# A low-half score product on 64 partitions instead of 128

## Chip, cores and metric

One Trainium2 chip, one core. The time is device microseconds of one launch, the median of several runs; lower is better. All matrix products run on TensorE (PE in the profile, its weight loads PEld), everything elementwise on VectorE (DVE), ScalarE (ACT) and GpSimd (POOL); transfers are queued by SyncE (SP).

## What is computed

A decoder trunk of two layers over 1024 tokens of width 1024. Each layer has a mixer (RMSNorm, one input projection, dilated sliding-window attention beside stick-breaking attention, gates, output projection) and a gated feed-forward block. The edit lies in the dilated attention: twelve heads of width 64 in three groups with (window, dilation) of (128, 1), (512, 4) and (2048, 16).

```python
DSW_GROUPS = ((128, 1), (512, 4), (2048, 16))
DSW_HEADS_PER_GROUP = 4
...
scores = jnp.einsum('brhnqc,brhnkc->brhnqk', qs, kw).astype(jnp.float32) * (hd ** -0.5)
...
scores = jnp.where(valid, scores + bias, -jnp.inf)
mx = jnp.max(scores, axis=-1, keepdims=True)
p = jnp.exp(scores - mx)
den = jnp.sum(p, axis=-1, keepdims=True)
o = jnp.einsum('brhnqk,brhnkc->brhnqc', p, vw) / den
```

The score product contracts over c, the head width of 64.

## The kernel before

All products are made in a rounded fp32 type (F32R) from a high and a low part: a number x is split into hi, the rounded value, and lo = x - hi, and a product is hi·hi + hi·lo + lo·hi. For dense products these are three matmuls (lines 1014 to 1016, for example). For scores, where only 64 of the 128 partitions would be filled, two parts share one matmul. The helper `scores(o, qt, ql, k)` (line 643) makes two matmuls into the same PSUM tile: its first (line 644) takes as k a tile with k's high part on partitions 0 to 63 and k's low part on 64 to 127, and as qt the high part of q on both halves, so that it sums hi·hi and hi·lo; its second (line 645) takes the low part of q on partitions 0 to 63 and zeros on 64 to 127, so that it adds lo·hi. The first argument behind the output is the stationary operand (128 partitions x 128 columns, loaded by an LDWEIGHTS record), k is the moving one.

Three kinds of attention item call this helper: `stick_item` (stick-breaking), `near_item` (dilation 1) and `far_item` (the two dilated groups together). The last is the one concerned. There are 16 far items a layer (i from 0 to 15), each for one head slot and one residue of the sequence, with both groups g = 0, 1. Their operands lie in a tile `t_kq` of shape [128, g, 3, 256]; the middle index is k (0), q high (1), q low (2). Two such tiles alternate (`R["kq", i % 2]`). `fetch_kq(i)` (line 866) fills one from a scratch tensor `tk` in HBM with three transfers on SP's queue: one for partitions 0 to 63 (line 872: k high, q high, q low) and one for each group on partitions 64 to 127 (line 874: k low, q high). The third column block of partitions 64 to 127 is never transferred. It is set to zero by a memset on POOL (line 870), once for each of the two tiles, in the first two fetches of a layer.

The function `score` inside `far_item` (line 889) makes an item's eight matmuls one behind the other, with nothing between them: for each g the pair of lines 644 and 645 on 128 key columns into bank z0 (line 899), then for each g the pair on 256 key columns into bank z1 (line 901). VectorE then adds the bias and takes the maximum (line 913, read as a minimum since signs are turned), ScalarE exponentiates (line 914). Later calls transpose the probabilities (lines 921 to 923) and multiply by the values (lines 931 and 933).

TensorE's list is written by hand order: `manual_schedule` keeps the order of the program text. A generator object `Dense` holds the layer's dense products (projections for gates, q, k and v: lines 1014 to 1016) and hands them out in between; `attend` calls an item's score, then dense pieces, then its transposes and value products, at a fixed rate for each kind of item. So the order on TensorE is fixed when the program is built. `fetch` asks for t_kq of item i when item i - 2 has been scored. Two further lines matter as a comparison: line 2120 transposes five small parameter arrays of 8, 16, 66, 22 and 8 rows once a layer, and line 839 transposes a tile of 32 columns.

Of the kernel before, what the change touches and what calls it, by code (L numbers as in the profile page):

```python
# [16 lines left out]
P = 128  # L17
# [39 lines left out]
def f32(ap):  # L57
    return ap.bitcast(F32)
# [3 lines left out]
def trunk_kernel(ctx, tc, x, norm1, w_in, b_gate, w_br, w_o, norm2, w_up, conv_w, conv_b, w_down, norm_f, out, depth=None, probe=None):  # L62
    nc = tc.nc
    act, dve, pe, pool = nc.scalar, nc.vector, nc.tensor, nc.gpsimd
# [60 lines left out]
    def bank(tag, name):  # L125
        return ps.tile([P, 512], F32, tag=tag, name=name)
# [95 lines left out]
    class Dense:  # L222
# [43 lines left out]
        def fetch(self):  # L266
# [28 lines left out]
            while self.kq < self.scored + 2 and there(self.kq):  # L295
                fetch_kq(self.kq)
                self.at(LEAD_T if self.kq > 1 else LEAD - 2 * self.kq, lambda i=self.kq: self.done.add(f"F{i}"))
                self.kq += 1
# [343 lines left out]

    def scores(o, qt, ql, k):
        pe.matmul(o, qt, k, start=True, stop=False, skip_group_check=True)
        pe.matmul(o, ql, k, start=False, stop=True, skip_group_check=True)

    def parts(src, n, name):

        hi, lo = small(name + "h", F32R), small(name + "l", F32R)
        with tc.high_priority(offset=AHEAD):  # L650
            split(hi[:, :n], lo[:, :n], src[:, :n], "is")
        return hi, lo

    def fold(dst, o):

        n = o.shape[-1]
        tmp = small("fold")
        with tc.high_priority(offset=AHEAD):
            act.copy(tmp[0:64, :n], o[64:128, :])
            dve.tensor_tensor(dst, o[0:64, :], tmp[0:64, :n], ALU.add)  # L660
# [205 lines left out]
    def fetch_kq(i):  # L866

        if i < 2:
            t = R["kq", i] = sb.tile([P, 2, 3, 256], F32R, tag="xa", bufs=4, name="t_kq")
            pool.memset(f32(t[64:128, :, 2, :]), 0.0)  # L870
        t, there = R["kq", i % 2], tk[i // 8][i // 4 % 2, :, i % 4]
        nc.sync.dma_start(f32(t[0:64]), there[:, :, 1:4, :])
        for g in range(2):
            nc.sync.dma_start(f32(t[64:128, g, 0:2, :]), there[:, g, 0:3:2, :])
# [5 lines left out]
    def far_item(dense, pr, s, r, share):  # L880
        i = 8 * pr + 4 * s + r
        slot = 2 * pr + s
        if s == 0 and r == 0:
            R["st1", pr] = sb.tile([P, 2, 2, 2, 4], F32, tag="st1", bufs=2, name="st1")
            R["ot", pr] = None
        st = R["st1", pr]
        shared = {}

        def score():
            if r == 0:  # L890
                bias = share["bias"] = sb.tile([P, 2, 256], F32, tag="bias", name="bias1")
                dve.tensor_scalar(bias[:, 0, :], base0, 4.0 * SLOPES[4 + slot], None, ALU.mult)
                dve.tensor_scalar(bias[:, 1, :], base2, 4.0 * SLOPES[8 + slot], None, ALU.mult)
            bias = share["bias"]
            pt = shared["p"] = sb.tile([P, T], F32, tag="p4", bufs=4, name="p1")
            z0, z1 = bank("s", "z10"), bank("s", "z11")
            t = R["kq", i % 2]
            for g in range(2):
                scores(z0[:, P * g : P * g + P], t[:, g, 1, 0:P], t[:, g, 2, 0:P], t[:, g, 0, 0:P])
            for g in range(2):  # L900
                scores(z1[:, 256 * g : 256 * g + 256], t[:, g, 1, P:256], t[:, g, 2, P:256], t[:, g, 0, :])
            dense.scored = i + 1
            if (s, r) == (1, 0):
                near_stats(pr)
            for n in range(2):
                flat = pt[:, 256:768] if n else pt[:, 0:256]
                if n:
                    zz, pp, bb = z1, flat, bias.rearrange("p g c -> p (g c)")
                else:
                    zz, pp, bb = z0[:, 0:256].rearrange("p (g c) -> p g c", g=2), flat.rearrange("p (g c) -> p g c", g=2), bias[:, :, P:256]  # L910
                nm = st[:, 0, s, n, r : r + 1]
                with tc.high_priority(offset=AHEAD):
                    LAST["red"] = dve.tensor_tensor_reduce(pp, zz, bb, 1.0, 3e38, ALU.add, ALU.min, nm).ins.name
                    act.activation(flat, flat, AF.Exp, bias=nm, scale=-1.0, accum_out=st[:, 1, s, n, r : r + 1])
            if (s, r) == (1, 3):
                factors(pr)

        def turn(g):
            pt = shared["p"]
            tp = bank("t", "t1")  # L920
            pe.transpose(tp[:, 0:P], pt[:, P * g : P * g + P], ident)
            pe.transpose(tp[:, P : 2 * P], pt[:, 256 + 256 * g : 384 + 256 * g], ident)
            pe.transpose(tp[:, 2 * P : 3 * P], pt[:, 384 + 256 * g : 512 + 256 * g], ident)
            shared[g] = parts(tp, 384, "p1")

        def apply(g):
            if r % 2 == 0 and g == 0:
                share["o"] = bank("o", "o1")
            o, oc, vt = share["o"], 256 * (r % 2), R["v", i][:, g]
            for p in (0, 1):  # L930
                pe.matmul(o[:, oc : oc + 256], vt[:, 0:P], shared[g][p][:, 0:256], start=(r % 2 == 0 and g == 0 and p == 0), stop=False, skip_group_check=True)
            for p in (0, 1):
                pe.matmul(o[:, oc + P : oc + 256], vt[:, P:256], shared[g][p][:, 256:384], start=False, stop=(r % 2 == 1 and g == 1 and p == 1), skip_group_check=True)
            if g == 1:
                dense.applied = i + 1
            if r % 2 == 1 and g == 1:
                if R["ot", pr] is None:
                    R["ot", pr] = sb.tile([P, T], F32, tag="ot", name="ot")
                fold(R["ot", pr][64 * s : 64 * s + 64, 512 * (r // 2) : 512 * (r // 2) + 512], o)
                if s == 1 and r == 3:  # L940
                    join(dense, pr)

        return [score], [(lambda g=g: turn(g), lambda g=g: apply(g)) for g in range(2)]

    def near_stats(pr):
        sn = R["sn", pr] = sb.tile([P, 2, 2, 2, 4], F32, tag="sn", bufs=1, name="sn")
        nc.sync.dma_start(sn.rearrange("j a s n r -> j (a s) n r"), tok_view(dn[pr]))

    def factors(pr):

        sn, st = R["sn", pr], R["st1", pr]
        nat, far_ = (t.rearrange("j a s n r -> j a (s n r)") for t in (sn, st))
        w = sb.tile([P, 6, 16], F32, tag="sw", bufs=1, name="sw")
        f = R["f", pr] = sb.tile([P, 2, 2, 2, 4], F32, tag="sf", bufs=1, name="sf")
        ff = f.rearrange("j a s n r -> j a (s n r)")
        dve.tensor_tensor(w[:, 0, :], nat[:, 0, :], far_[:, 0, :], ALU.min)
        dve.tensor_tensor(w[:, 1, :], w[:, 0, :], nat[:, 0, :], ALU.subtract)
        dve.tensor_tensor(w[:, 2, :], w[:, 0, :], far_[:, 0, :], ALU.subtract)
        act.activation(w[:, 1:3, :], w[:, 1:3, :], AF.Exp)
        dve.tensor_tensor(w[:, 3, :], w[:, 1, :], nat[:, 1, :], ALU.mult)  # L960
        dve.tensor_tensor(w[:, 4, :], w[:, 2, :], far_[:, 1, :], ALU.mult)
        dve.tensor_tensor(w[:, 3, :], w[:, 3, :], w[:, 4, :], ALU.add)
        dve.reciprocal(w[:, 5, :], w[:, 3, :])
        dve.tensor_tensor(ff[:, 0, :], w[:, 1, :], w[:, 5, :], ALU.mult)
        dve.tensor_tensor(ff[:, 1, :], w[:, 2, :], w[:, 5, :], ALU.mult)

        R["fx", pr] = []
        for a in range(2):
            fx = sb.tile([P, 2, 4, 2, 64], F32, tag="p4", bufs=4, name="fx")
            for s in range(2):  # L970
                act.copy(fx[:, :, :, s, :], f[:, a, s, :, :].unsqueeze(3).to_broadcast([P, 2, 4, 64]))
            R["fx", pr].append(fx.rearrange("p n r s c -> p n r (s c)"))
# [1178 lines left out]
```

## Time and profile before

| | us |
|---|---|
| median of 3 runs (2620.66 to 2622.22) | 2621.4 |
| profiled execution, own time | 2621.54 |
| its span, first to last instruction | 2619.8 |

The profile is one execution. It lists, for each engine, instructions with start and length. A matmul's record runs from its start to a modelled end and overlaps those of its neighbours, so distances between starts tell more than lengths. In a record like "128*128 128x256" the first pair is rows x columns of the stationary operand, the second the moving one. "q<-p" names the tile written and those read; "<-" behind an idle time names what ended it. TensorE's clock as granted is 1.00 over the whole span.

### The profile page before, as it was taken

To read this page: it belongs to the slowest core of one execution; us is meant where nothing else is said; L and a number is where in the kernel's file an instruction comes from. 1 tells how busy PE (TensorE), PEld (TensorE's weight loads), DVE (VectorE), ACT (ScalarE), POOL (GpSimd) and SP (SyncE) were. 2 spreads that over 40 slices of the span, in tenths; PEclk is the share of its full clock that TensorE was granted. 3 is DMA by queue.
4 is the path that set the end of the run, shared out by engine and by line. 5 is a ranking of instruction groups with operands and counts; after the bars stand their busy time and mean duration, and the time that the engine had idled before them with its cause. 6 is when DMAs were issued, how large, how long until landed. Compare 5 with 4: busy or idle time off the path is not lost.

```text
span 2619.8 us, 36195 instructions
## 1 busy us (share of the span) xinstructions
PE 2606.3 (99%) x12732; PEld 2185.4 (83%) x12732; DVE 2089.1 (80%) x3485; ACT 1358.8 (52%) x2533; POOL 100.4 (4%) x135
## 2 busy tenths in 40 slices
PE   9999999999999999999999999999999999999999
PEld 8888888888888888888888888888888888888887
DVE  8877777795988888897677778777869888889965
ACT  6555666574554555422445555666645555544225
POOL 3000000030000000000000000000300000000000
PEclk9999999999999999999999999999999999999999
DMA  7434578873344444688344436787633344446962
GB/s 255 152 117 135 163 202 219 212 245 93 93 145 154 143 169 137 240 325 311 145 150 141 129 124 187 198 224 212 209 97 116 129 156 150 147 167 257 347 240 112
DMA packets 400418, 468.22 MB, mean 179 GB/s; under 512 B 24309, under 2 KB 315501, under 8 KB 398445
## 3 DMA queue, kind: packets, MB, share of 16 engines
q1 hardware_dynamic: 400220, 465.90, 55.1%
q8 instruction: 101, 1.65, 0.3%
q14 instruction: 81, 0.66, 0.1%
q10 hardware_dynamic: 16, 0.00, 0.0%
HBM read 303.23 MB, written 162.59 MB: 178 GB/s over the span
## 4 chain that ended last, share of the span: by engine, by line
PE 94%; DVE 2%; ACT 2%; DMA 1%; issue 1%; SPq 0%; POOL 0%; DVEq 0%; ACTq 0%; POOLq 0%
PE u_a L1014 6%; PE u_a L1016 6%; PE u_a L1015 6%; PE d_ps L1763 5%; PE d_ps L1764 5%; PE d_ps L1765 5%; PE i_a L1014 5%; PE i_a L1016 4%; PE i_a L1015 4%; PE u_c L1014 3%; PE u_c L1016 3%; PE u_c L1015 3%; PE i_c L1014 2%; PE i_c L1016 2%; PE i_c L1015 2%; PE o_ps L182 2%
## 5 line engine op out<-in xcount | busy, mean ns | idle before, releaser
L141 ACT CAST w_hi<-up_a 128x512 fp32r<-128x512 f32 x280 | 174.0, 622 | 277.1 <-DVE up_a L1617 120.6
L148 DVE TENSOR_TENSOR w_lo<-up_a,w_hi 128x512 fp32r<-128x512 f32 x280 | 189.6, 689 | 83.4 <-ACT w_hi L141 83.4
L141 ACT CAST w_hi<-in_a 128x512 fp32r<-128x512 f32 x252 | 156.1, 622 | 163.4 <-PE i_c L1015 38.3
L148 DVE TENSOR_TENSOR w_lo<-in_a,w_hi 128x512 fp32r<-128x512 f32 x252 | 173.0, 688 | 74.9 <-ACT w_hi L141 65.8
L1771 DVE TENSOR_TENSOR x<-x,d_ps 128x512 f32<-128x512 f32 (+1 forms) x228 | 153.8, 676 | 64.9 <-PE d_ps L1765 61.5
L1763 PE MATMUL d_ps<-gd_in,w_hi 128*128 128x512 f32 (+1 forms) x340 | 130.1, 383 | 0.0
L1764 PE MATMUL d_ps<-gd_in,w_hi 128*128 128x512 f32 (+1 forms) x340 | 129.9, 382 | 0.0
L1765 PE MATMUL d_ps<-gd_in,w_lo 128*128 128x512 f32 (+1 forms) x340 | 129.9, 382 | 0.0
L1014 PE MATMUL u_a<-t_hi,w_hi 128*128 128x512 f32 x320 | 124.6, 389 | 0.0
L1016 PE MATMUL u_a<-t_hi,w_lo 128*128 128x512 f32 x320 | 124.6, 389 | 0.0
L1015 PE MATMUL u_a<-t_lo,w_hi 128*128 128x512 f32 x320 | 124.6, 389 | 0.0
L1016 PE MATMUL u_a<-hh,w_lo 128*128 128x512 f32 x320 | 124.6, 389 | 0.0
L1014 PE MATMUL u_a<-hh,w_hi 128*128 128x512 f32 x320 | 124.6, 389 | 0.0
L1015 PE MATMUL u_a<-hl,w_hi 128*128 128x512 f32 x320 | 124.6, 389 | 0.0
L1014 PE MATMUL i_a<-hh,w_hi 128*128 128x512 f32 x288 | 119.2, 414 | 0.0
L1014 PE MATMUL i_a<-t_hi,w_hi 128*128 128x512 f32 x288 | 118.4, 411 | 0.0
L1763 PE MATMUL d_ps<-gd_in,wd 128*128 128x512 f32 (+1 forms) x292 | 114.0, 390 | 0.0
L1016 PE MATMUL i_a<-hh,w_lo 128*128 128x512 f32 x288 | 113.2, 393 | 0.0
L1016 PE MATMUL i_a<-t_hi,w_lo 128*128 128x512 f32 x288 | 113.1, 393 | 0.0
L1015 PE MATMUL i_a<-t_lo,w_hi 128*128 128x512 f32 x288 | 113.0, 392 | 0.0
L1765 PE MATMUL d_ps<-gd_in,wd 128*128 128x512 f32 (+1 forms) x292 | 112.9, 387 | 0.0
L1764 PE MATMUL d_ps<-gd_in,wd 128*128 128x512 f32 (+1 forms) x292 | 112.9, 387 | 0.0
(379 smaller groups left out, 7839.6 us busy)
## 6 DMA issues: line engine op xcount, KB each, us to landing
gd<-g SPq DMA_DIRECT2D x154, 512.0 KB, 3.3
gd_in<-gd SPq DMA_DIRECT2D x154, 512.0 KB, 6.2
up_a<-in_w_up_dram SPq DMA_DIRECT2D x80, 512.0 KB, 5.3
in_a<-in_w_in_dram SPq DMA_DIRECT2D x72, 512.0 KB, 5.4
wd_raw<-in_w_down_dram SPq DMA_DIRECT2D x22, 1024.0 KB, 11.2
gin<-gs SPq DMA_DIRECT2D x32, 512.0 KB, 4.3
w_raw<-in_w_o_dram SPq DMA_DIRECT2D x64, 256.0 KB, 2.9
gs<-u SPq DMA_DIRECT2D x48, 256.0 KB, 4.0
```

What stands on the lines that cost most here:

```text
L141: one = act.copy(hi, src)
L148: two = dve.tensor_tensor(lo, src, f32(hi), ALU.subtract)
L182: pe.matmul(o, lh, rh, start=(first and i == 0), stop=False, skip_group_check=share)
L1014: pe.matmul(o, w[0][:, c], rh, start=(first and i == 0), stop=False, skip_group_check=True)
L1015: pe.matmul(o, w[0][:, c], rl, start=False, stop=False, skip_group_check=True)
L1016: pe.matmul(o, w[1][:, c], rh, start=False, stop=(last and i == 3), skip_group_check=True)
L1763: pe.matmul(o[:, sub], wh[:, c], gh[:, sub], start=(i == 0 and k in (0, 4, 5)), stop=False, skip_group_check=True)
L1764: pe.matmul(o[:, sub], wh[:, c], gl[:, sub], start=False, stop=False, skip_group_check=True)
L1765: pe.matmul(o[:, sub], wl[:, c], gh[:, sub], start=False, stop=(i == m - 1), skip_group_check=True)
L1771: dve.tensor_tensor(x, x, o[:, sub], ALU.add)
```

## The change

The second matmul of `scores` takes as many partitions of k as its stationary operand has. The far items hand in q's low part on partitions 0 to 63 alone, so their second product contracts over 64 partitions. The zeros beside it are no longer read, and the memset is left out. The other two kinds of item still hand in 128 partitions. Later line numbers go down by one.

```diff
     def scores(o, qt, ql, k):
         pe.matmul(o, qt, k, start=True, stop=False, skip_group_check=True)
-        pe.matmul(o, ql, k, start=False, stop=True, skip_group_check=True)
+        pe.matmul(o, ql, k[0 : ql.shape[0]], start=False, stop=True, skip_group_check=True)
...
             t = R["kq", i] = sb.tile([P, 2, 3, 256], F32R, tag="xa", bufs=4, name="t_kq")
-            pool.memset(f32(t[64:128, :, 2, :]), 0.0)
...
             for g in range(2):
-                scores(z0[:, P * g : P * g + P], t[:, g, 1, 0:P], t[:, g, 2, 0:P], t[:, g, 0, 0:P])
+                scores(z0[:, P * g : P * g + P], t[:, g, 1, 0:P], t[0:64, g, 2, 0:P], t[:, g, 0, 0:P])
             for g in range(2):
-                scores(z1[:, 256 * g : 256 * g + 256], t[:, g, 1, P:256], t[:, g, 2, P:256], t[:, g, 0, :])
+                scores(z1[:, 256 * g : 256 * g + 256], t[:, g, 1, P:256], t[0:64, g, 2, P:256], t[:, g, 0, :])
```

## The prediction

> **What bounds the kernel now.** I read the page first: busy times, the granted clock, and the chain of waits that ended last.
>
> ```profile
> span 2619.8 us, 36195 instructions
> PE 2606.3 (99%) x12732; PEld 2185.4 (83%) x12732; DVE 2089.1 (80%) x3485; ACT 1358.8 (52%) x2533; POOL 100.4 (4%) x135
> PEclk9999999999999999999999999999999999999999
> PE 94%; DVE 2%; ACT 2%; DMA 1%; issue 1%; SPq 0%; POOL 0%; DVEq 0%; ACTq 0%; POOLq 0%
> ```
>
> TensorE sets the end: busy 99% of the span, 94% of the chain, at full clock. That average need not hold where the edit lies, so the table by stretches came next, cut at the first and the last score product of the dilated heads in each layer.
>
> ```profile
> 412.40:495.10 82.70, 81.83 (x486) 70.85 (x485) 61.27 (x135) 50.28 (x115) 0.52 (x1) 1.00 0.87 220
> 1705.80:1814.90 109.10, 107.10 (x639) 92.98 (x638) 79.92 (x179) 63.80 (x149) 0.52 (x1) 1.00 0.85 216
> ```
>
> The columns are length, then busy time of PE, PEld, DVE, ACT and POOL, clock and DMA share. In these 191.8 us TensorE is idle 0.87 + 2.00 = 2.87 us. So here, too, a microsecond more or less on TensorE is a microsecond of the total, except for what those 2.87 us can take up. The rows of the line and tile say what that idle time waits for, and how many products are touched:
>
> ```profile
> L645 PEld LDWEIGHTS z<-t_kq x128: 187/192/193, 412.5 to 1814.4; 128*128 128x128 f32 x128
> L645 PE MATMUL z<-t_kq x128: 272/278/287, 412.5 to 1814.5; 128*128 128x128 f32 x64, 128*128 128x256 f32 x64
>   DMA t_kq<-tk: 2.3, 3
> L870 POOL MEMSET t_kq<- x4: 522/522/523, 398.6 to 1712.4; 64x512 f32 x4
> ```
>
> So 128 second products, half of them 128 columns wide and half 256: 32 calls of a score function with four each. Most of the idle time is t_kq's transfers.
>
> **What an item costs today.** The timeline of the first one, matmuls and then weight loads (start, length of the record, engine):
>
> ```profile
> 412.25 0.39 PE L1016 MATMUL i_b<-hh,w_lo 128*128 128x512 f32 x1
> 412.48 0.22 PE L644 MATMUL z<-t_kq 128*128 128x128 f32 x1
> 412.54 0.28 PE L645 MATMUL z<-t_kq 128*128 128x128 f32 x1
> ...
> 413.28 0.28 PE L645 MATMUL z<-t_kq 128*128 128x256 f32 x1
> 413.40 0.40 PE L1014 MATMUL i_b<-hh,w_hi 128*128 128x512 f32 x1
> 412.48 0.19 PEld L645 LDWEIGHTS z<-t_kq 128*128 128x128 f32 x1
> 412.59 0.19 PEld L644 LDWEIGHTS z<-t_kq 128*128 128x128 f32 x1
> 412.70 0.19 PEld L645 LDWEIGHTS z<-t_kq 128*128 128x128 f32 x1
> ```
>
> Records overlap, so starts are what count. From the first product's start to the next dense product's start there are 413.40 - 412.48 = 0.92 us for eight products. Each load starts while the product before it is still streaming (412.48, with the first product) and they follow each other at 0.11 us: the narrow products are paced by loads, and each load is hidden behind another one's streaming. This overlap is what the edit touches.
>
> **Edit 1: second product with 64 rows.** The order on TensorE, ACT, DVE and SP stays as it is; only the 128 products of line 645 on t_kq shrink from 128 to 64 rows, in the stationary and the moving operand. Columns, and so the streamed elements, are the same. For what rows are worth the trace has one place, the ten transposes of line 2120 with 8, 16, 22 or 66 rows. Loads of layer 1 (after the 256-column product of line 184, and with no wait on a transfer), and the like place in layer 0 after a 512-column one:
>
> ```profile
> 1357.29 0.28 PE L184 MATMUL v_ps<-v_w,hl 128*128 128x256 f32 x1
> 1357.50 0.13 PEld L2120 LDWEIGHTS pt_c<-ident,raw_c 8*128 8x128 f32 x1
> 1357.72 0.14 PEld L2120 LDWEIGHTS pt_c<-ident,raw_c 66*128 66x128 f32 x1
> 1357.92 0.13 PEld L2120 LDWEIGHTS pt_c<-ident,raw_c 22*128 22x128 f32 x1
> 1357.98 0.14 PEld L2120 LDWEIGHTS pt_c<-ident,raw_c 8*128 8x128 f32 x1
> 1358.14 0.19 PEld L1014 LDWEIGHTS i_a<-hh,w_hi 128*128 128x128 f32 x1
> 1358.25 0.19 PEld L1015 LDWEIGHTS i_a<-hl,w_hi 128*128 128x128 f32 x1
> 64.00 0.39 PE L184 MATMUL q_ps<-hh,kq_w 128*128 128x512 f32 x1
> 64.32 0.13 PEld L2120 LDWEIGHTS pt_c<-ident,raw_c 8*128 8x128 f32 x1 [0.35 <-issue]
> ```
>
> Two things are to be seen. First, a load of 8 rows and one of 66 have the same length (0.13 and 0.14): fewer rows save nothing. Second, wherever the number of rows passes from many to few or back, the overlap is gone. After the 256-column product the load comes 1357.50 - 1357.29 = 0.21 us behind its start, after the 512-column one 64.32 - 64.00 = 0.32, whereas in the item above it comes at once. From 66 rows to 22 there are 0.20 us, from 8 back to 128 0.16, but from 22 to 8, both few, 0.06. The two distances 0.21 and 0.32 differ by 256 columns, 0.11 us, which is the streaming; what is left, 0.10, is a fixed stretch in which the array runs empty. And the first full load after it is no longer hidden: 1358.25 - 1358.14 = 0.11 until its product streams and the next load may start.
>
> I take 64 rows as "few", because 22 and 66 rows stand on different sides of the step and in the built programs the changed products ask for a 64-row tile, the 22-row ones for 32, those of 66 rows for all 128. That is the choice on which all hangs, since no row has 64.
>
> In the changed item each of the eight products is then followed by a change of height: 64 after 128 four times, 128 after 64 four times (the last one at the dense product behind the item). Each costs its own streaming plus the empty stretch (0.21 for 256 columns as measured; 0.21 - 0.055 = 0.155 for 128), and an exposed load of 0.11 behind it. Sum: 4 x 0.155 + 4 x 0.21 + 8 x 0.11 = 0.62 + 0.84 + 0.88 = 2.34 us in place of 0.92, so +1.42 an item, and 32 x 1.42 = +45.4 us.
>
> Bounds of this term. Below: the load runs ahead into the empty stretch after all, and only that stretch is paid: 4 x 0.155 + 4 x 0.21 = 1.46, +0.54 an item, +17 us. Lowest: no step at 64 rows, 0. Above: the 66-row transpose keeps the next load away for 0.20 us although it streams only 66 columns (0.03 at 0.11 for 256) behind a load that, by the 0.06 from 22 rows to 8, takes some 0.03: the empty stretch is then 0.14 instead of 0.10, 256 x 0.04 = 10 us more, +55 us. I take 45.4, since its two terms come from products and loads of the same type as these; the 66-row row is a transpose.
>
> The Trainium skill says in "TensorEngine Tiling (Array Packing)", section Key Properties, that changing the tiling mode, not just the tile, drains TensorE. It is the rule that speaks against this change; it gives no price. By it every change of tile shape would cost, and the sum would stand; the trace agrees for rows (0.21 and 0.32 above) but shows a change of columns that costs nothing (next fence), by which the sum would be 0.
>
> **Edit 2: the memset goes.** Four of 0.52 us on POOL, which is 4% busy. The first, at 398.6, ends 13 us before the first score product at 412.48; no wait for POOL shows at that line. Hidden behind the dense products of these 13 us, so 0; were that cover gone, at most 4 x 0.52 = 2.1 us. SP's queue keeps its transfers in their order, and t_kq's do not write the rows that the memset wrote.
>
> **Where the stall goes.** The consumers (the DVE reduction of line 913, ACT's exponential, the transposes) are called up later on TensorE's own list, behind dense products in the same order, so they are late by as much as TensorE itself. Transfers gain time: the 2.3 us of waiting for t_kq may shrink. Part of that is fetched only when earlier products are done, so I give back 1.
>
> **Sum.** The profiled execution took 2621.54 us (span 2619.8 plus 1.7 around it), 0.1 above the median of 2621.4. 2621.5 + 45.4 - 1 = 2666 us, 1.7% slower. A difference under 0.2%, 5 us, can't be told from none.
>
> **Rivals.**
>
> *No step at 64 rows.* What speaks for it is the one other tile shape in the trace, the transpose of line 839 on 32 of 128 columns, beside a full one (line 923):
>
> ```profile
> 418.73 0.09 PEld L839 LDWEIGHTS st_t<-ident,st 128*32 128x32 f32 x1
> 418.76 0.19 PEld L1014 LDWEIGHTS i_a<-hh,w_hi 128*128 128x128 f32 x1
> 418.87 0.19 PEld L1015 LDWEIGHTS i_a<-hl,w_hi 128*128 128x128 f32 x1
> 420.69 0.14 PEld L923 LDWEIGHTS t<-ident,p 128*128 128x128 f32 x1
> 420.80 0.19 PEld L1014 LDWEIGHTS i_a<-hh,w_hi 128*128 128x128 f32 x1
> 420.90 0.19 PEld L1015 LDWEIGHTS i_a<-hl,w_hi 128*128 128x128 f32 x1
> ```
>
> The dense load follows the odd one by 0.03, the full one by 0.11, and the next load comes 0.11 and 0.10 after: nothing is drained. If rows behaved so at 64, the item stays at 0.92 and the time is 2621, not slower than before, and within the 2.1 us of the memset on either side. It decides as soon as a 64-row load starts with the product before it. Against it stand all the row changes of line 2120. 8%.
>
> *Only the empty stretch is paid*, the load being hidden in it: 2621.5 + 17 = 2639. The 0.11 at 1358.14 speaks against it: there the product begins a full load behind its own load's start. 8%. The skill's "TensorE: Matmul & The Clock Gate", section Step-by-step, lets a load be pulled ahead where it goes to the background weight buffer; by that this case, or the one before, would hold. The trace agrees for equal shapes (412.48) and not for changed heights.
>
> *The stage takes it up.* If transfers paced it (DMA share 0.87 and 0.85), longer products would only fill waits. With 2.87 us of idle time it can't be more than that: 2621.5 + 45.4 - 2.9 = 2664, inside the forecast's own range, 5 of its 83%.
>
> *Smaller is faster.* Half the rows could halve the 15 us that 128 second products at some 0.12 take: 2614. Loads of 8 and 66 rows being equally long leave this 1%.
>
> **Chances.** Forecast 83%, its own range 2650 to 2680 (both ends of the empty stretch, 0.06 to 0.14 on 256 changes; 0.04 less is 10 us). With the 2639 case inside, 2636 to 2680 leaves out the 9% of no step and faster and little above. Slower by over 0.2%: 91%; within 0.2%: 8%; faster: 1%.
>
> **What would show it.** Right: on the line of the second product the form reads 64*128; within an item a load starts 0.15 to 0.16 us behind a 128-column product's start and 0.21 behind a 256-column one's, with 0.11 more until the product streams; an item spans 2.3 us instead of 0.92; the two stages are about 23 us longer each, everything else the same. Wrong: loads of 64 rows that start along with the product before them, an item under 1.0 us, or a stage that grows by far less than its sixteen items do.

## The result, and the profile after

| | before | changed |
|---|---|---|
| median, us | 2621.4 (2620.7 to 2622.2, 4 runs) | 2666.4 (2662.0 to 2667.9, 4 runs) |
| profiled execution, us | 2621.54 | 2662.03 |
| its span, us | 2619.8 | 2660.3 |

The ratio is 1.0169 with a 95% interval of 1.0157 to 1.0182: 1.7% slower. The profiled execution of the changed kernel happens to be the fastest of its four, 4.3 us under the median. What lies between is dealt with below, at the clock.

The page of the changed kernel answers to the first lines of the prediction:

```profile
span 2660.3 us, 36181 instructions
PE 2647.7 (100%) x12732; PEld 2199.5 (83%) x12732; DVE 2090.9 (79%) x3485; ACT 1362.3 (51%) x2533; POOL 99.9 (4%) x131
PE 96%; ACT 1%; DMA 1%; DVE 1%; issue 0%; SPq 0%; DVEq 0%; ACTq 0%
```

VectorE and ScalarE have the work they had; TensorE is busy 41.4 us longer with as many instructions as before. Where, the table of stretches shows for both kernels, cut at the first far item of a layer and at the dense product behind its last (length, then busy time of PE, PEld, DVE, ACT, POOL, clock, DMA share). Before:

```profile
412.50:520.10 107.60, 106.73 (x638) 92.90 (x636) 80.15 (x177) 63.85 (x148) 0.52 (x1) 1.00 0.85 219
1705.80:1814.60 108.80, 106.80 (x637) 92.72 (x636) 79.71 (x177) 63.69 (x148) 0.52 (x1) 1.00 0.85 216
```

After:

```profile
413.10:541.60 128.50, 128.45 (x641) 101.27 (x640) 82.43 (x181) 66.30 (x151) 0.00 (x0) 1.00 0.70 184
1726.20:1855.30 129.10, 127.53 (x638) 100.45 (x636) 81.65 (x178) 66.20 (x150) 0.00 (x0) 1.00 0.70 183
```

The stretch of layer 0 ends a little late here: its last item begins at 538.43 and the dense product behind it at 540.65 (below), which makes 127.5 us in place of 107.6. Layer 1 has 129.1 in place of 108.8. The two stages hold 40 of the 40.5 us that separate the two profiled executions. (In the prediction the stretch of layer 0 was cut at 495, four items short; its idle time, 0.87 us, is the same up to 520.)

What grew in there, the first item shows. Its matmuls in the changed kernel, and its weight loads:

```profile
412.89 0.39 PE L1015 MATMUL i_b<-hh,w_lo 128*128 128x512 f32 x1
413.12 0.22 PE L644 MATMUL z<-t_kq 128*128 128x128 f32 x1
413.27 0.32 PE L645 MATMUL z<-t_kq 64*128 64x128 f32 x1
...
414.97 0.38 PE L645 MATMUL z<-t_kq 64*128 64x256 f32 x1
415.28 0.50 PE L1013 MATMUL i_b<-hh,w_hi 128*128 128x512 f32 x1
```

```profile
412.89 0.19 PEld L644 LDWEIGHTS z<-t_kq 128*128 128x128 f32 x1
413.27 0.18 PEld L645 LDWEIGHTS z<-t_kq 64*128 64x128 f32 x1 [0.19 <-issue]
413.52 0.19 PEld L644 LDWEIGHTS z<-t_kq 128*128 128x128 f32 x1
413.78 0.18 PEld L645 LDWEIGHTS z<-t_kq 64*128 64x128 f32 x1
414.03 0.19 PEld L644 LDWEIGHTS z<-t_kq 128*128 128x128 f32 x1
414.34 0.18 PEld L645 LDWEIGHTS z<-t_kq 64*128 64x128 f32 x1
...
415.27 0.19 PEld L1013 LDWEIGHTS i_b<-hh,w_hi 128*128 128x128 f32 x1
415.38 0.19 PEld L1014 LDWEIGHTS i_b<-hl,w_hi 128*128 128x128 f32 x1
```

The first product's load still runs ahead, along with the dense product (both at 412.89). Every later load waits. The first 64-row load comes 0.15 us behind the start of its forerunner; after that loads follow each other at 0.25 to 0.26 us around products of 128 columns and at 0.31 around 256, where it was 0.11 and 0.12. The load of the dense product behind the item is exposed, too: 0.11 us from 415.27 to 415.38. In all 2.27 us from 413.12 to the streaming of the dense product, in place of 0.92.

### The profile page after: what moved, and what is told of

Its sections match the earlier page's. It is cut to its first block, busy times and chain, and to the rows that moved or that the text cites. A ratio compares the mean times of both kernels' runs of the same rounds, so it can differ in the third digit from the quotient of the medians.

```text
span 2660.3 us, 36181 instructions
## 1 busy us (share of the span) xinstructions
PE 2647.7 (100%) x12732; PEld 2199.5 (83%) x12732; DVE 2090.9 (79%) x3485; ACT 1362.3 (51%) x2533; POOL 99.9 (4%) x131
## 4 chain that ended last, share of the span: by engine, by line
PE 96%; ACT 1%; DMA 1%; DVE 1%; issue 0%; SPq 0%; DVEq 0%; ACTq 0%
PE u_a L1013 5%; PE u_a L1014 5%; PE u_a L1015 5%; PE d_ps L1762 5%; PE d_ps L1764 5%; PE d_ps L1763 5%; PE i_a L1013 5%; PE i_a L1015 5%; PE i_a L1014 5%; PE u_c L1013 3%; PE u_c L1015 3%; PE u_c L1014 3%; PE i_c L1013 2%; PE i_c L1015 2%; PE i_c L1014 2%; PE z L645 2%
```

## The experiments

Ten runs follow, eight kernels and two repeats, in three sets, each set beside runs of the kernel before on the same chip. "Height" is the number of rows of the tile of TensorE's array that a product asks for. It stands in the built program, not in the profile, which prints a product's rows alone: in the changed program the 128 second products ask for 64 rows, in the one with 96 rows below for 128.

**The rows alone, memset kept.**

```diff
             t = R["kq", i] = sb.tile([P, 2, 3, 256], F32R, tag="xa", bufs=4, name="t_kq")
+            pool.memset(f32(t[64:128, :, 2, :]), 0.0)
```

(against the changed kernel)

> The 64-row second product alone; the memset of line 870 is kept. If the whole loss is the change of tile height on TensorE: 2662 to 2668 us, as the changed kernel, and an item of eight products spans 2.15 to 2.25 us. If the missing memset (another release of the tile, another time of the first transfers) had any part in it: the time lies nearer to 2621, by that part. If the 64-row product is slow in itself: 2662 to 2668 as well, so this run does not tell those two apart.

Measured: 2665.07 us (2661.78 to 2668.28), ratio 1.0165 (1.0150 to 1.0180). The changed kernel had 2666.36, and 2665.07 when it was run again (below). The fastest runs, at a granted clock of 1.000, are 2661.78 us with the memset and 2661.20 and 2662.03 without it. The memset has no part in the loss that these runs could show.

**Fewer changes of height, the same products.** Both kernels differ from the changed one in the order within an item only.

```diff
-            for g in range(2):
-                scores(z0[:, P * g : P * g + P], t[:, g, 1, 0:P], t[0:64, g, 2, 0:P], t[:, g, 0, 0:P])
-            for g in range(2):
-                scores(z1[:, 256 * g : 256 * g + 256], t[:, g, 1, P:256], t[0:64, g, 2, P:256], t[:, g, 0, :])
+            many = []
+            for zz, c, qc, kc in ((z0, P, slice(0, P), slice(0, P)), (z1, 256, slice(P, 256), slice(0, 256))):
+                for g in range(2):
+                    many.append((zz[:, c * g : c * g + c], t[:, g, 1, qc], t[0:64, g, 2, qc], t[:, g, 0, kc], g))
+            for some in (many,):
+                for o, qt, ql, k, g in some:
+                    pe.matmul(o, qt, k, start=(g == 0), stop=False, skip_group_check=True)
+                for o, qt, ql, k, g in some:
+                    pe.matmul(o, ql, k[0:64], start=False, stop=(g == 1), skip_group_check=True)
```

The four-change kernel has `(many[:2], many[2:])` in place of `(many,)`.

> The changed kernel, with an item's four 128-row products first and its four 64-row products behind them: two changes of height an item in place of eight. If each change costs the empty stretch and an exposed load (both behind a 256-column product here, 0.31 us from start to start in place of 0.12): 2 x 0.19 x 32 = +12 us, 2632 to 2637. If a 64-row product is slow in itself, whatever stands beside it, by (2666 - 2621) / 128 = 0.35 us: no gain from the order, 2660 to 2668.

> The changed kernel, with the two 128-row and then the two 64-row products of each score bank: four changes of height an item. Change of height: two behind 128-column products (0.255 in place of 0.11) and two behind 256-column ones (0.31 in place of 0.12): 0.67 us an item, +21 us, 2640 to 2646, between the two-change kernel and the changed one. 64-row product slow in itself: 2660 to 2668.

Measured: 2631.16 us (2630.05 to 2634.56), ratio 1.0038 (1.0024 to 1.0053), with two changes; 2643.56 us (2641.81 to 2647.55), ratio 1.0085 (1.0070 to 1.0100), with four. Over the 2621.28 of before in the same set that is +9.9 and +22.3, and the changed kernel with its eight has +44 to +45 (40.5 between the profiled executions, at full clock). The median with two changes lies 0.8 us under the range that was expected; two of the four runs with four changes, 2644.99 and 2647.55 us, had a mean clock of 0.998 and 0.997, so their median, too, holds some of the scatter dealt with below. The same 128 products of 64 rows are in all three, so the rival by which they are slow in themselves falls. The first item of the two-change kernel, products of one line taken together:

```profile
412.70 0.62 PE L903 MATMUL z<-t_kq 128*128 128x128 f32 x4
413.26 0.72 PE L905 MATMUL z<-t_kq 64*128 64x128 f32 x4
413.91 0.50 PE L1018 MATMUL i_b<-hh,w_hi 128*128 128x512 f32 x1
413.25 0.52 PEld L905 LDWEIGHTS z<-t_kq 64*128 64x128 f32 x4
```

From 412.70 to 413.91 are 1.21 us, and some 0.11 of exposed load behind: 1.32, 0.40 over the 0.92 of before, where 0.38 was expected. The four 64-row loads take 0.52 us together, with records of 0.18, so they follow each other at 0.11 again: within a group of four, loads hide. By the items alone 32 of them would add some 12 us; 9.9 came.

**The grouped order without a change of height.** Line 905's counterpart on `t[:, g, 2, qc]` and the whole of k, memset kept: the kernel before in another order. It was run twice.

> The kernel before with the order of the two-change kernel (an item's four first products, then its four second ones), all on 128 rows and with the memset. No change of height, so no price: 2619 to 2624, an item of 0.9 to 1.0 us. If the order by itself moved the time (a score bank that VectorE gets later, or a saving that made the two-change kernel look cheaper than it is), it shows here as a difference of several us from 2621.

> All products on 128 rows in the grouped order, once more, since its median lay 1.5 us under that of the kernel before. Its items take the same 0.92 us, so the price of the order is nil: 2619 to 2623 and an interval of the ratio that holds 1. If the grouped order is really faster: a median under 2620 again and an interval wholly under 1.

Measured: 2619.62 us (2617.92 to 2622.22), ratio 0.9995 (0.9985 to 1.0004), and 2620.07 (2618.35 to 2621.30), ratio 0.9993 (0.9984 to 1.0002). The first item is 0.92 us long, as before. The order by itself costs nothing. Both medians lie 1.2 to 1.5 us under that of before, and ten of the eleven runs of the repeat lie under that median, but both intervals hold 1, so a gain isn't shown; one of this size would account for most of what the two-change kernel fell short of its items. No kernel of this study is shown to be faster than the one before.

**96 rows, order as before.**

```diff
+            pool.memset(f32(t[64:96, :, 2, :]), 0.0)
...
-                scores(z0[:, P * g : P * g + P], t[:, g, 1, 0:P], t[0:64, g, 2, 0:P], t[:, g, 0, 0:P])
+                scores(z0[:, P * g : P * g + P], t[:, g, 1, 0:P], t[0:96, g, 2, 0:P], t[:, g, 0, 0:P])
...
-                scores(z1[:, 256 * g : 256 * g + 256], t[:, g, 1, P:256], t[0:64, g, 2, P:256], t[:, g, 0, :])
+                scores(z1[:, 256 * g : 256 * g + 256], t[:, g, 1, P:256], t[0:96, g, 2, P:256], t[:, g, 0, :])
```

> The second product on 96 partitions (64 with data, 32 set to zero by a memset), order as before. If the price hangs on the tile height, which is 128 rows for 96 as for 66: no change, 2619 to 2624, and an item of 0.92 us. If fewer rows than the neighbour has are what costs, whatever the tile: the full price, 2660 to 2668, or, by rows left out, about half, 2640 to 2645.

Measured: 2621.68 us (2620.62 to 2625.24), ratio 1.0001 (0.9992 to 1.0010). Its first item:

```profile
412.88 0.22 PE L644 MATMUL z<-t_kq 128*128 128x128 f32 x1
412.94 0.28 PE L645 MATMUL z<-t_kq 96*128 96x128 f32 x1
...
413.80 0.40 PE L1014 MATMUL i_b<-hh,w_hi 128*128 128x512 f32 x1
```

0.92 us, although the two products have different numbers of rows (the form reads 96*128). Not fewer rows cost, but rows few enough for another tile; where between 64 and 96 the step lies, no run here shows. The Trainium skill's "TensorEngine Tiling (Array Packing)", section Key Properties, puts it that way: switching the tiling mode drains the engine. Here 96 beside 128 rows, one mode by the heights in the built program, cost 0 and 64 beside 128, two modes, some 0.16 us a switch (40.5 us on 256 of them).

**The same edit in another kind of item.** The kernel before, with the second product of the dilation-1 heads on 64 rows:

```diff
-                scores(zz, *(q[:, m, x, j * P : j * P + P] for x in range(2)), k[:, (b - 1) * P + c : b * P + P])
+                scores(zz, q[:, m, 0, j * P : j * P + P], q[0:64, m, 1, j * P : j * P + P], k[:, (b - 1) * P + c : b * P + P])
```

> The kernel before, with the 64-row second product in the other kind of item instead, the heads of dilation 1: 64 pairs in all, 8 of them with 128 columns and 56 with 256, far items untouched. By the starts in the changed kernel's trace a pair of 256 columns takes 0.63 in place of 0.235 us and one of 128 columns 0.51 in place of 0.22: 56 x 0.39 + 8 x 0.29 = +24 us, 2642 to 2649. If the price were something of the far items (their tile, their transfers, their place in the layer): 2619 to 2624.

Measured: 2645.12 us (2643.61 to 2645.62), ratio 1.0090 (1.0073 to 1.0107), +24.0 us over the 2621.16 of its set, as forecast from the changed kernel's starts. Two pairs of it:

```profile
336.80 0.28 PE L644 MATMUL z<-kv,slots 128*128 128x256 f32 x1
337.00 0.38 PE L645 MATMUL z<-kv,slots 64*128 64x256 f32 x1
337.32 0.38 PE L644 MATMUL z<-kv,slots 128*128 128x256 f32 x1
337.63 0.38 PE L645 MATMUL z<-kv,slots 64*128 64x256 f32 x1
337.94 0.50 PE L1014 MATMUL i_a<-hh,w_hi 128*128 128x512 f32 x1
```

0.31 to 0.32 us from start to start, as in the far items; the price goes with the change of height and not with the place.

**The scatter: TensorE's clock.** Runs of the changed kernel lie up to 7 us apart, those of the kernel before up to 4. Each run lists its mean granted clock, and the two go together: in the first four runs of the changed kernel 2662.03 us went with 1.000, 2665.66 with 0.998, and 2667.05 and 2667.88 with 0.997. The profile of the kernel with the rows alone fell on a run of 2667.09 us at 0.997. Its stretches around the second far item of layer 1 show the clock in the third column from the right:

```profile
1744.00:1750.00 6.00, 4.28 (x14) 2.68 (x13) 1.43 (x4) 1.15 (x4) 0.00 (x0) 0.82 0.26 65
1750.00:1756.00 6.00, 6.00 (x15) 3.94 (x15) 1.61 (x6) 2.65 (x6) 0.00 (x0) 0.50 0.45 109
1756.00:1762.00 6.00, 6.00 (x19) 4.84 (x20) 2.92 (x6) 1.77 (x4) 0.00 (x0) 0.54 0.69 169
1762.00:1768.00 6.00, 6.00 (x30) 4.62 (x29) 4.68 (x12) 3.00 (x7) 0.00 (x0) 1.00 0.42 108
```

and its timeline just before the fall a wait with a stretched item behind it:

```profile
1746.71 0.30 PE L644 MATMUL z<-t_kq 128*128 128x128 f32 x1 [1.72 <-DMA t_kq<-tk]
1746.93 0.32 PE L645 MATMUL z<-t_kq 64*128 64x128 f32 x1
...
1748.06 0.58 PE L645 MATMUL z<-t_kq 64*128 64x256 f32 x1
```

From 1748 on records are half as long again; the clock stays at 0.5 almost to the end of the third row, some 13.6 us by stretches of one microsecond, though dense products come at once behind the item. In the profiled execution of the changed kernel the same wait (1.55 us) was followed by no fall. To see whether the wait is what lets it fall, it was filled:

```diff
             t = R["kq", i % 2]
+            if i == 1 and LAST["layer"] == 1:
+                for _ in range(7):
+                    pe.matmul(z0, H[0][0][:, 0, 0:P], H[0][0][:, 0, :], start=True, stop=True, skip_group_check=True)
```

(`LAST["layer"]` is set where a layer's mixer begins.) Beside it the changed kernel ran once more, as it is.

> The changed kernel with seven additional dense matmuls of 512 columns (their result is overwritten) ahead of the second far item of layer 1, where TensorE otherwise waits 1.6 to 1.7 us for t_kq. In the trace of the kernel with the rows alone the granted clock fell to 0.5 for some 11 us right behind that wait; in that of the changed kernel it did not, and the times lie apart by about 5 us (2662 and 2667). If the wait together with the stretched item behind it lets the clock fall: no run shows a clock below 0.998, the median is 2660 to 2664 and the runs lie within 3 us. If the fall has another cause: the same spread as before, 2662 to 2668, median 2665 or more, by up to 1.6 us more for the additional products.

> The changed kernel once more, beside the one with the filled wait on the same chip: runs between 2661 and 2669, those with a clock of 1.0 or 0.999 at 2661 to 2664 and those with 0.997 or 0.998 at 2665 to 2669. If the scatter has nothing to do with the clock, times and clocks do not go together.

Measured: the changed kernel again 2665.07 us, four runs: 2661.20 (1.000), 2662.66 (0.999), 2667.48 and 2667.85 (0.997 both). So the scatter goes with the clock. But the filled kernel had 2662.64 (1.000), 2668.47 (0.998), 2670.60 and 2671.57 (0.997 both), median 2669.54: the expectation that filling this wait ends the falls failed. Its profile, one of the 0.997 runs, shows why: no fall at the filled item of layer 1 any more, but one in layer 0, at the same item there.

```profile
432.00:436.00 4.00, 3.42 (x12) 2.36 (x13) 1.13 (x4) 0.84 (x3) 0.00 (x0) 0.98 0.20 51
436.00:440.00 4.00, 4.00 (x11) 2.51 (x9) 1.12 (x3) 2.42 (x6) 0.00 (x0) 0.50 0.52 121
440.00:444.00 4.00, 4.00 (x12) 3.09 (x13) 1.91 (x4) 0.83 (x3) 0.00 (x0) 0.50 0.55 155
444.00:448.00 4.00, 4.00 (x18) 3.34 (x17) 2.34 (x4) 1.39 (x3) 0.00 (x0) 0.74 0.69 162
```

There the waits for t_kq were only 0.36 and 0.23 us, within an item of 2.6 us whose loads are all exposed, and the fall lasted some 10.2 us. (The same trace has a third place, outside the attention: 3.4 us at half clock from 2070.8 on, behind a wait of 2.5 us for ScalarE.) The theory was widened to both places of the far items, and tested by `if i == 1:`, which fills layer 0's wait as well:

> The changed kernel with the seven additional dense matmuls ahead of the second far item of both layers, not of layer 1 alone. In the trace of the kernel filled in layer 1 only, the clock fell to 0.5 for some 10 us in layer 0 instead, behind two waits of 0.4 and 0.2 us at that layer's second far item, and not in layer 1. If waits at the second far item, together with the stretched items there, are what lets it fall: no run under 0.998, all runs at 2662 to 2666 (up to 1.6 us of additional matmuls in layer 0, where less waiting is there to hide them). If the stretched items alone are enough: clocks of 0.997 and times of 2668 to 2672 go on in about half of the runs.

Measured: five runs, all at clock 1.000, 2663.64 to 2664.96, median 2664.77. The spread is 1.3 us in place of 6 to 7, and no run shows a mean clock under 1.000, where five of the eight runs of the changed kernel had 0.998 or 0.997. So by these five runs the gaps at the second far item of the two layers are where most of the falls start. The fourteen added matmuls (1.6 us for seven at 432.10 to 433.68) make these runs some 2 to 3.5 us longer than those of the changed kernel at 0.999 or 1.000.

A wait alone can do it, too, but briefly. The first run of the grouped order on 128 rows, with no change of height, had a wait of 1.76 us at the same item; its stretches behind it:

```profile
1724.00:1726.00 2.00, 0.94 (x7) 0.84 (x7) 0.00 (x0) 0.00 (x0) 0.00 (x0) 1.00 0.05 17
1726.00:1728.00 2.00, 2.00 (x9) 1.67 (x8) 1.04 (x4) 1.35 (x4) 0.00 (x0) 0.64 0.08 17
1728.00:1730.00 2.00, 2.00 (x9) 1.81 (x9) 0.71 (x2) 1.08 (x3) 0.00 (x0) 0.51 0.83 228
1730.00:1732.00 2.00, 2.00 (x13) 1.69 (x13) 2.00 (x6) 1.64 (x5) 0.00 (x0) 1.00 0.33 93
```

Half the clock for some 3.4 us, an estimated 1.7 us lost. The profile of the four-change kernel has a fall of the same length (1736.5 to 1740.0, behind a wait of 1.7 us). The falls seen in the profiles with eight changes of height are one such stretch long (3.4, the second run of the changed kernel and the late one of the filled kernel), three (10.2) or four (13.6). The first of these, in the second run of the changed kernel:

```profile
1748.00:1749.00 1.00, 1.00 (x4) 0.58 (x4) 0.15 (x3) 0.60 (x2) 0.00 (x0) 0.85 0.00 0
...
1752.00:1753.00 1.00, 1.00 (x4) 0.66 (x4) 0.76 (x2) 0.40 (x2) 0.00 (x0) 0.94 0.09 15
```

Why does a fall come in one execution and not in the next, with nearly equal waits (1.55 us without, 1.58 with one)? The traces answer it in part. In all twelve, every stretch between two changes of the clock is a whole multiple of 3.413 us, whatever TensorE does in it: in the kernel with the rows alone 510 of them at full clock, 4 at half, 264 at full, up to the fall with which every trace ends once the last product is done (in the kernel before at 2618.8, in the last microsecond of its span). So changes come only at the ends of windows of this length, and where the windows lie against the instructions differs from one execution to the next.

How full a window is of streaming can be estimated from the matmul records, at 0.227 us for 512 columns at full clock and 0.427 at half, as the dense products' starts show. Between the first 20 us of a trace and its last product the window ahead of each of the six falls is filled to 0.20 to 0.42; every other window at full clock is filled more, the emptiest to just over 0.42. At half clock, the clock stayed low behind windows filled to 0.55 to 0.76 and rose behind those of 0.81 and more. In the two executions above the window with the wait is filled to 0.47 (1743.95 to 1747.37, dense products ahead of the wait) and to 0.20 (1745.30 to 1748.71, the stretched item behind it). A stretched item streams little in its time: by this it can both bring on a fall and prolong it. That is read from traces; no run tried it by itself, and no profile with fewer than eight changes shows a long fall.

## Why the prediction was right, point by point

**TensorE bounds the stage: right.** 40 of the 40.5 us lie in the two stages, and consumers add nothing: DVE and ACT are busy as long as before. The prediction said 23 us a stage; it is 20.

**Change of height, 1.42 us an item: right in mechanism, mis-sized by a twentieth.** Each product was put at its streaming plus 0.10 plus a load of 0.11, that is 0.265 and 0.32 us; the trace has 0.25 to 0.26 and 0.31, so the empty stretch is some 0.09. That makes 2.27 in place of 2.34 an item, +1.35, or 43.2 us in place of 45.4. Twelve of the 32 items are followed by transposes, whose exposed load lengthens the first record by 0.06 (0.33 us in place of 0.27, line 920) and not by the 0.11 of a dense product: 0.6 less, 42.6. The choice on which all hung, that 64 rows stand with 22 and not with 66, holds: 64 beside 128 pays, 96 beside 128 doesn't.

**The lower bound, only the empty stretch paid (2639): wrong,** the load is seen behind it, 0.11 us at 415.27. **No step at 64 rows (2621): wrong**; it is what happens at 96. **Smaller is faster: wrong**, a 64-row load has a record of 0.183 us against 0.192, and 64-row products of 128 and 256 columns lie as far apart (0.25 and 0.31) as the 128-row ones between them. **The stage takes it up (2664):** only in part; the idle time of the two stages went from 2.87 to 1.62 us.

**The memset at nothing: right** (2661.78 us with it and 2661.20 without, each the fastest run; that both medians read 2665.07 is chance, since they hold the scatter).

**Giving back 1 us of waits: near in size, wrong in place.** From the list of TensorE's waits, those in the far items before:

```profile
PE z L644 <- DMA t_kq<-tk: 1.8, 2, 1.5
PE o L931 <- DVE p1l L148: 1.3, 4, 0.5
PE o L931 <- ACT p1h L141: 0.4, 2, 0.2
```

and after, with one more that the list of before doesn't have:

```profile
PE z L644 <- DMA t_kq<-tk: 1.6, 1, 1.6
PE o L930 <- DVE p1l L148: 0.4, 2, 0.2
PE v_ps L182 <- ACT hh L141: 0.6, 1, 0.6
```

The wait for t_kq stays (1.8 to 1.6); it is VectorE's and ScalarE's probabilities that come in time now (1.3 + 0.4 to 0.4). In all 1.5 us. 42.6 - 1.5 = 41.1, against 40.1 in the two stages (19.9 and 20.2); where the other 1.0 us went isn't located. The one more, of the last line, lies in the first 54 us, ahead of all that the edit touches, and the second run of the changed kernel doesn't have it: its 0.6 us is a difference between executions, and with it TensorE's idle time over the whole span shrinks by no more than 0.9 us (13.5 to 12.6).

**The number itself owes something to chance.** 2666 stands beside a median of 2666.4. At a mean clock of 0.999 or 1.000 the changed kernel takes 2661.2 to 2662.7, by which the sum was 4 us too high. The falls of the clock, which the prediction didn't have, come with 3 to 6 us more in five of eight runs, and bring the median up to it. That 2666 and 2666.4 agree to half a microsecond is luck; that the change costs some 40 us by its changes of height is not.

## What to carry to other kernels

Zeros that pad a product to the height of its neighbours can be worth keeping: in these traces, narrow products follow each other with hidden loads only as long as they ask for a tile of the same height. Before narrowing a product, look at what stands beside it, and count changes of height, not rows saved; if narrow ones are wanted, group them (two changes an item cost a quarter of what eight did). In a trace the sign is a weight load that starts behind, not along with, the product before it.

## What was not expected

The clock. Waits of 1.6 to 2.5 us, and in one case of 0.36 and 0.23 us within a stretched item, were followed by 3.4 to 13.6 us at half the clock. The kernel before waits 1.5 us at the same place, and its profiled execution shows no fall there. The Trainium skill's "TensorE: Matmul & The Clock Gate", section What's actually happening, knows only the full and the half clock, set by how busy TensorE was in a freely running window of some 3.4 us. The 0.50 agrees with it, and so do the lengths, one, three and four times 3.41 us, and the multiples of 3.413 us between all changes, whose place against the instructions differs between executions. The section's condition of a whole idle window does not agree: the longest wait ahead of one of these falls was 2.5 us, and the windows ahead of them still held 0.20 to 0.42 of streaming.
